# A two-layer decoder trunk: decay levels recorded four to a run, the second layer opened by the values of two groups, output pages split into other places and earlier

## The chip, the cores and the metric

The kernel runs on one core of one Trainium2 chip. The metric is the device time of one execution in microseconds (us). The engines are named as the profile names them: PE (TensorE, the matrix engine) with its weight loads PEld, DVE (VectorE), ACT (ScalarE), POOL (GpSimd), and SP (SyncE), whose queue issues every DMA of this kernel.

## The reference, cut to what matters

The input `x` has 1024 tokens of 1024 features. Layer A is gated linear attention with 4 heads (key width 128, value width 256), layer B is dilated sliding-window attention with 8 query heads in 3 groups over one shared set of keys and values. Each layer ends in an output projection, a residual and a layer norm.

```python
# layer A, per head, written chunk by chunk
b = cumsum(log_a)                                  # decay, log space, within a chunk
att[i, j] = sum_d q[i,d] * k[j,d] * exp(b[i,d] - b[j,d])      # j <= i
o = att @ v + (q * exp(b)) @ state
x1 = layer_norm(ALPHA * x + ((o / rms(o)) * g_norm * silu(g)) @ w_out)
# layer B
k, v = split(x1 @ w_kv)                            # 3 groups x 2 kv heads x 128
q, g = split(x1 @ w_in)
o_g = softmax over a band (windows 128, 512, 2048; dilations 1, 4, 16) per group
o = sum over groups of softmax(lse_g) * o_g
out = layer_norm(ALPHA * x1 + (o * silu(g)) @ w_out)
```

All of it is float32. The kernel gets float32 accuracy out of faster float32r matmuls by splitting each operand into a high and a low page (`split_hi` on ACT, `split_lo` on DVE or POOL) and issuing three matmuls, high by high, high by low and low by high.

## The kernel before, in words

Nothing is issued where it is written. Every call is recorded as an operation of a small scheduler, `Sched`, with a priority (its place in the text, moved by `S.later`), the engines that may run it (`S.vp` is DVE or POOL, `S.va` DVE or ACT) and an estimated cost. `Sched.order` then lets the operation that can start earliest go next, engine by engine, with buffers of a pool handed out in order. So an edit of the text changes the order on all engines, also far from the edit, and the order is fixed when the program is built. All instructions of the trace carry the helper's line, L452; tiles are told by their names.

Stages on PE, with the names of the tiles that it writes:

- Prologue, 1.25 to 29.9 us: values of head 0 and the gate's low rank (`pro`), while `x` arrives in tiles `xf` (tag `X`, 3 buffers) and is split to `xh`, `xl`.
- Layer A, to 337.8 us. Per head: projections of q, k and g (`acc`, 128x512), the gate (a matmul into `lv`, then `mn` on DVE and a scan into `b`), `levels`, `state_prep` (four-wide transposes of `ke` into `ms`), `chunks` (`po`, `ms`).
- Output projection of layer A with its layer norm, `out_ln(0, ...)`, first for tokens 0 to 511, then for 512 to 1023; it writes the pages `x1h`, `x1l` of layer B. The norm's two sums over features are pairs of matmuls with a page of ones, `ms<-sum,onesr`.
- Layer B, from 431.4 us: `layer_b` projects values and keys, then loops over 8 units (heads) with `scores`, `q_proj`, `g_proj`, `attend`, `close`.
- Output projection of layer B: tokens 0 to 511 by feature blocks (`out_ln(1, ...)`, banks `acc`, `lv`, `po` in turn), tokens 512 to 1023 by rows (`out_ln_rows`, weights `woh`, `wol`).

What the change touches:

- `levels(h)`, line 899. The attention matrix of a chunk is put together from eight small pieces: `k` against `q` for the diagonal, and for each L of 64, 32, ..., 1 a tile `X` that DVE, POOL and ACT fill (two subtractions, an exponential, two products), multiplied with itself. The products are float32 matmuls that use 32 columns of the array at a time (the trace writes them `128*32`, two records each). Two pieces at a time go into one bank, `lv` (2 buffers), as one group, so PE has four such groups per head, and DVE and ACT move each bank on to `Dg` and `AT`.
- `layer_b(xs)`, from line 1174. It starts with `proj_v0(range(4))`: values of group 0, four blocks of 128 tokens, each block a 256-wide `acc` accumulated over all eight pages of `x1`. `proj_v(0)` follows: values of groups 1 and 2 for tokens 0 to 511, four banks (`lv`, `lv`, `po`, `po`) at once, so that each page of `x1` is used by 12 matmuls of 512 columns before the next is needed.
- The end, lines 1553 to 1574. The gated output of each unit, `og`, is written to memory (`ogB`) for units 0 to 5, read back after the last `g_proj` through staging tiles `ogf` (tag `a`, 13 buffers, shared with the score tiles `P`) and split to `ogh`, `ogl` in pool `p1`, 16 pages that the `x1` pages leave. The weight pages `woh`, `wol` of the row part lie in pool `p0`.

Of the kernel before, what the change touches and what calls it, by code (L numbers as in the profile page):

```python
# [7 lines left out]
F32 = mybir.dt.float32  # L8
# [589 lines left out]
def trunk(tc, xT, wP, wA, wA12, wAv3, w2, wO, wK, wV0, wV12, wB, wOB, par_d,  # L598
# [13 lines left out]
    def split_hi(dst, src):  # L612
        S.scalar.activation(dst, src, AF.Copy)
# [4 lines left out]
    def page(pool, dt, name):  # L618
        return pool.tile([128, T], dt, name=name, tag="pg", bufs=16)

    def hs(half):
        return slice(half * 512, half * 512 + 512)
# [94 lines left out]
    def og_page(kt, pool):  # L717
        while kt >= len(ogs):
            n = len(ogs)
            a = page(pool, FR, f"ogh{n}")  # L720
            b = page(pool, FR, f"ogl{n}")
            ogs.append((a, b))
        return ogs[kt]

    def layer_a(t2, t1, after):
# [13 lines left out]
        S.vector.memset(smask.rearrange("p (n c) -> p n c", c=128)[:, :, 0:1], 0.0)  # L739

        def xtile(dt, name, shape=(128, T)):
            return t1.tile(list(shape), dt, name=name, tag="X", bufs=3)

        H = [dict() for _ in range(GH)]
        xs = []
# [137 lines left out]
        def gate(h):  # L883
            b = t1.tile([128, T], F32, name="b", tag="b", bufs=2)
            H[h]["b"] = b
            for half in range(2):
                r = hs(half)
                z = ps.tile([128, 512], F32, name="lv", bufs=2)
                S.tensor.matmul(z, w2t[:, h * 128:h * 128 + 128], aT[:, r], start=True, stop=True)
                sp = t1.tile([128, 512], F32, name="sp", bufs=2)  # L890
                S.scalar.activation(sp, z, AF.Abs, bias=b2c[:, h:h + 1])
                S.scalar.activation(sp, sp, AF.Exp, scale=-1.0)
                S.scalar.activation(sp, sp, AF.Ln, bias=onec)
                mn = t1.tile([128, 512], F32, name="mn", bufs=2)
                S.vector.tensor_scalar(mn, z, b2c[:, h:h + 1], 0.0, op0=OP.add, op1=OP.min)
                S.vp.tensor_sub(mn, mn, sp)
                S.vector.tensor_tensor_scan(b[:, r], smask, mn, 0.0, op0=OP.mult, op1=OP.add)

        def levels(h):
            q, k, b = H[h]["q"], H[h]["k"], H[h]["b"]  # L900
            AT, Dg = ATs[h % 2], Dgs[h % 2]
            pair = []

            for li in (NLEV - 1, *range(NLEV - 1)):
                if li < len(LEVELS):
                    L = LEVELS[li]
                    n = T // (2 * L)
                    X = xtile(F32, "X")
                    view = lambda t: t.rearrange("p (n s l) -> p n s l", s=2, l=L)
                    bv, Xv = view(b), view(X)  # L910
                    ref = bv[:, :, 0, L - 1:L].to_broadcast([128, n, L])
                    S.vector.tensor_sub(Xv[:, :, 1, :], bv[:, :, 1, :], ref)
                    S.vp.tensor_sub(Xv[:, :, 0, :], ref, bv[:, :, 0, :])
                    S.scalar.activation(X, X, AF.Exp, scale=1.0 / 16.0)
                    S.vector.tensor_mul(Xv[:, :, 1, :], Xv[:, :, 1, :], view(q)[:, :, 1, :])
                    S.vp.tensor_mul(Xv[:, :, 0, :], Xv[:, :, 0, :], view(k)[:, :, 0, :])
                    lt, rt = X, X
                else:
                    L = 0
                    lt, rt = k, q  # L920


                pair.append((li, L, lt, rt))
                if len(pair) < 2:
                    continue
                pb = ps.tile([128, 2, 256], F32, name="lv", bufs=2)
                with S.group():
                    for i, (_, L, lt, rt) in enumerate(pair):
                        for c in range(NCH):
                            o = c * 128  # L930
                            if L == 64:

                                for s in (0, 32):
                                    d = c % 2 * 64 + s
                                    S.tensor.matmul(pb[d:d + 32, i, c // 2 * 64:c // 2 * 64 + 64],
                                                     lt[:, o + s:o + s + 32], rt[:, o + 64:o + 128],
                                                     start=True, stop=True)
                                continue
                            for s in (0, 64) if L == 32 else range(0, 128, 32):
                                e = s + 32 if L == 32 else s  # L940
                                S.tensor.matmul(pb[s:s + 32, i, c * 32:c * 32 + 32], lt[:, o + s:o + s + 32],
                                                 rt[:, o + e:o + e + 32], start=True, stop=True)
                for i, (lj, L, _, _) in enumerate(pair):
                    if L == 64:
                        pl = pb[:, i].rearrange("p (c q) -> p c q", q=64)
                        AP = AT.rearrange("p (c two) i -> p two c i", two=2)
                        for x in range(2):
                            S.va.copy(AP[0:64, x, :, 64:128], pl[x * 64:x * 64 + 64])
                        continue
                    pl = pb[:, i].rearrange("p (c q) -> p c q", q=32)  # L950
                    if L == 32:
                        for s in (0, 64):
                            S.va.copy(AT[s:s + 32, :, s + 32:s + 64], pl[s:s + 32])
                    else:
                        S.vector.copy_predicated(
                            Dg, lmask[:, lj - 2:lj - 1, :].to_broadcast([128, NCH, 32]), pl)
                pair = []
            for s in range(0, 128, 32):
                S.va.copy(AT[s:s + 32, :, s:s + 32], Dg[s:s + 32])
# [91 lines left out]
    def small(name, tag, bufs, dt=F32, shape=(128, 512)):  # L1051
        return hp.tile(list(shape), dt, name=name, tag=tag, bufs=bufs)

    def load_og(src, kt, pool, stage, halves=(0, 1)):
        hi, lo = og_page(kt, pool)
        for half in halves:
            f = stage()
            S.sync.dma_start(f, src[:, hs(half)])
            split_hi(hi[:, hs(half)], f)
            split_lo(lo[:, hs(half)], f, hi[:, hs(half)])  # L1060
# [110 lines left out]
            return ap.rearrange("p (n a e) -> p n a e", n=4, a=8)  # L1171
        return ap.rearrange("p (i r) -> p i r", r=DIL[g])

    def layer_b(xs):
        bmask = hp.tile([128, 256], F32, name="bmask", bufs=1)
        S.sync.dma_start(bmask, bmask_d)
        rmask = hp.tile([128, 64], F32, name="rmask", bufs=1)
# [26 lines left out]
        def proj_v0(blocks):  # L1204
            for c in range(2):
                if V[c][0] is None:
                    V[c][0] = page(p0, F32, f"V{c}0")

            def evac(j, acc):
                S.scalar.activation(blk(V[0][0], j), acc[:, 0:128], AF.Copy)  # L1210
                S.vector.tensor_copy(blk(V[1][0], j), acc[:, 128:256])
            project_tok(wV0, xs, [(j, lambda x, j=j: blk(x, j)) for j in blocks], evac)
# [47 lines left out]
                S.sync.dma_start(x1t[i][:, et * 128:et * 128 + 128], blk(t, i))  # L1260


        proj_v0(range(4))
        proj_v(0)
        for g in range(3):
            for c in range(2):
                project(wK[2 * g + c], xs, lambda hf, acc, p=K[c][g]: rope(p, g, hf, acc))
# [40 lines left out]
        def g_proj(u):  # L1308
            sg = page(p0, F32, "sg")
            U[u]["sg"] = sg  # L1310

            def evac(half, acc):
                th = small("th", "t1", 2)
                S.scalar.activation(th, acc, AF.Tanh, scale=0.5)
                S.vector.scalar_tensor_tensor(sg[:, hs(half)], th, 1.0, acc, op0=OP.add, op1=OP.mult)
            project(wB[u, 3], xs, evac)
# [194 lines left out]
        for u in range(8):  # L1511
# [9 lines left out]
            if u == 3:  # L1521
                reload_kv()
        for u in (4, 5, 6, 7):
            g_proj(u)
            if u < 7:
                close(u)
# [22 lines left out]

    for half in range(2):  # L1550
        out_ln(0, hs(half), lambda et: load_w(wO[et]), lambda et: xT[et * 128:et * 128 + 128, :], emit_a)
    U = layer_b(x1s)

    ogs.clear()
    for kt in range(6):
        load_og(ogB[kt], kt, p1, lambda: small("ogf", "a", 13))
    for u in (6, 7):
        hi, lo = og_page(u, p1)
        for half in range(2):
            split_hi(hi[:, hs(half)], U[u]["og"][:, hs(half)])  # L1560
            split_lo(lo[:, hs(half)], U[u]["og"][:, hs(half)], hi[:, hs(half)])

# [4 lines left out]
    wo = []  # L1567
    for kt in range(NK):
        wf = wts.tile([128, 1024], F32, name="wf", bufs=2)
        hi, lo = page(p0, FR, "woh"), page(p0, FR, "wol")  # L1570
        with S.later(-EVAC):
            S.sync.dma_start(wf.rearrange("p (e c) -> p e c", e=NK), wOB[:, :, kt, :].rearrange("e p c -> p e c"))
            split_hi(hi, wf)
            split_lo(lo, wf, hi)
        wo.append((hi, lo))
# [96 lines left out]
```

## Time and profile before

| | us |
|---|---|
| median of 3 runs (1156.07 to 1156.78) | 1156.69 |
| the profiled execution's own time | 1157.39 |
| its span in the profile | 1155.6 |
| PE busy, share of the span | 1144.7, 99% |
| DVE busy | 808.5, 70% |
| ACT busy | 459.5, 40% |
| POOL busy | 199.6, 17% |
| first matmul of the program starts | 1.25 |
| last matmul of the program ends | 1148.0 |

The span is the stretch between the first and the last instruction of the profiled execution; 1.8 us lie around it. In a timeline row the first number is the start, the second the time from the start of its first to the end of its last instruction, both in us, and `x64` says that 64 records were merged. A matmul's own duration overlaps that of the next; what a matmul costs in a stream is the distance from its start to the next start. PE counts as busy while it is in such a stream, so a busy PE may still lose time: a distance longer than the usual one is how a wait or a change of work shows.

### The profile page before, as it was taken

How to read it: one execution, taken by the hardware profiler on the slowest of the kernel's cores; microseconds unless marked ns; L12 is line 12 of the kernel's file. 1: busy time of each engine (PE TensorE's matmuls, PEld its weight loads, DVE VectorE, ACT ScalarE, POOL GpSimd, SP SyncE). 2: the span in 40 equal slices, each digit the busy share in tenths (PEclk: the TensorE clock that was granted, in tenths of full speed). 3: DMA queues.
4: the chain of work that ended last, by engine and by line, in shares of the span. 5: the costliest groups of instructions: out<-in, count | busy, mean ns of one | idle time of the engine just before them, and what ended most of it. 6: DMA issues, size and time to landing. Idle time of an engine off the chain costs nothing.

```text
span 1155.6 us, 19794 instructions
## 1 busy us (share of the span) xinstructions
PE 1144.7 (99%) x7780; PEld 975.2 (84%) x7780; DVE 808.5 (70%) x1636; ACT 459.5 (40%) x965; POOL 199.6 (17%) x157
## 2 busy tenths in 40 slices
PE   9999999999999999999999999999999999999997
PEld 8888888889988888888888888888888888888876
DVE  6295952686966698765366868676778778768578
ACT  5354531545463335311214343434322433435242
POOL 1000000102111120221020314141222222204100
PEclk9999999999999999999999999999999999999999
DMA  8111122111144463643611211111151011124645
GB/s 266 59 39 37 67 81 86 43 57 46 66 170 135 141 199 134 200 135 111 210 37 38 56 38 56 38 40 53 38 165 39 20 39 37 39 75 146 199 129 183
DMA packets 93374, 108.40 MB, mean 94 GB/s; under 512 B 43648, under 2 KB 61952, under 8 KB 93280
## 3 DMA queue, kind: packets, MB, share of 16 engines
q1 hardware_dynamic: 93280, 107.13, 29.7%
q8 instruction: 61, 1.00, 0.4%
q14 instruction: 33, 0.27, 0.1%
HBM read 85.94 MB, written 21.17 MB: 93 GB/s over the span
## 4 chain that ended last, share of the span: by engine, by line
PE 93%; DVE 3%; DMA 2%; ACT 1%; issue 0%; SPq 0%; DVEq 0%
PE acc L452 63%; PE po L452 9%; PE lv L452 8%; PE vac L452 8%; PE ms L452 4%; PE pro L452 2%; DMA wf<-in_wOB 2%; DVE rt L452 1%; DVE wl L452 1%; DMA xf<-in_xT 1%; DVE wol L452 0%; DVE x1l L452 0%; ACT woh L452 0%; ACT wh L452 0%; SPq L452 0%
## 5 line engine op out<-in xcount | busy, mean ns | idle before, releaser
L452 PE MATMUL acc<-x1h,wh 128*128 128x512 f32 x608 | 252.1, 415 | 0.0
L452 PE MATMUL acc<-x1h,wl 128*128 128x512 f32 x608 | 237.6, 391 | 0.0
L452 PE MATMUL acc<-x1l,wh 128*128 128x512 f32 x608 | 237.0, 390 | 0.0
L452 ACT ACTIVATE wh<-wf 128x1024 fp32r<-128x1024 f32 (+2 forms) x104 | 108.2, 1041 | 260.9 <-PE acc L452 158.8
L452 POOL TENSOR_TENSOR wl<-wf,wh 128x1024 fp32r<-128x1024 f32 x43 | 102.9, 2394 | 564.3 <-ACT wh L452 366.9
L452 PEld LDWEIGHTS acc<-x1h,wl 128*128 128x128 f32 x608 | 114.1, 188 | 24.8
L452 PEld LDWEIGHTS acc<-x1l,wh 128*128 128x128 f32 x608 | 114.5, 188 | 21.3
L452 PEld LDWEIGHTS acc<-x1h,wh 128*128 128x128 f32 x608 | 114.4, 188 | 21.0
L452 ACT ACTIVATE P<-P,sts 128x128 f32<-128x128 f32 (+2 forms) x192 | 81.5, 425 | 121.8 <-DVE sts L452 121.4
L452 DVE TENSOR_TENSOR wl<-wf,wh 128x1024 fp32r<-128x1024 f32 (+2 forms) x62 | 76.9, 1240 | 57.7 <-ACT wh L452 45.6
L452 PE MATMUL acc<-xh,wh 128*128 128x512 f32 x256 | 101.9, 398 | 0.0
L452 PE MATMUL acc<-xh,wl 128*128 128x512 f32 x256 | 99.8, 390 | 0.0
L452 PE MATMUL acc<-xl,wh 128*128 128x512 f32 x256 | 99.7, 389 | 0.0
L452 DVE TENSOR_TENSOR t<-acc,cosT 128x512 f32<-128x512 f32 x60 | 41.3, 689 | 65.1 <-PE acc L452 65.0
L452 DVE TENSOR_TENSOR t<-acc,sinT 64x512 f32<-64x512 f32 x120 | 82.6, 688 | 1.6
L452 PE MATMUL lv<-K,Q 128*64 128x64 f32 (+2 forms) x512 | 69.4, 286 | 0.0
L452 DVE CUSTOM_DVE_ANT_0 P<-lv,bmask 128x256 f32<-128x256 f32 (+1 forms) x128 | 46.4, 379 | 29.3 <-PE lv L452 28.5
L452 DVE TENSOR_TENSOR Q<-t,t 128x512 f32<-128x512 f32 x44 | 61.7, 1402 | 1.3
L452 PEld LDWEIGHTS lv<-K,Q 128*128 128x128 f32 (+1 forms) x512 | 53.2, 163 | 10.0 <-issue 1.1
L452 PE MATMUL acc<-ogh,wh 128*128 128x512 f32 x152 | 60.2, 396 | 0.0
L452 PE MATMUL acc<-ogl,wh 128*128 128x512 f32 x152 | 59.2, 389 | 0.0
L452 PE MATMUL acc<-ogh,wl 128*128 128x512 f32 x152 | 59.2, 389 | 0.0
(251 smaller groups left out, 2227.8 us busy)
## 6 DMA issues: line engine op xcount, KB each, us to landing
wf<-in_wB SPq DMA_DIRECT2D x32, 512.0 KB
wf<-in_wA SPq DMA_DIRECT2D x24, 512.0 KB
wf<-in_wO SPq DMA_DIRECT2D x16, 512.0 KB
wf<-in_wOB SPq DMA_DIRECT2D x16, 512.0 KB
wf<-in_wV SPq DMA_DIRECT2D x12, 512.0 KB
res<-in_xT SPq DMA_DIRECT2D x16, 256.0 KB
x1d<-rt SPq DMA_DIRECT2D x16, 256.0 KB
out<-rt SPq DMA_DIRECT2D x16, 256.0 KB
```

What stands on the lines that cost most here:

```text
L452: getattr(handle[o.eng], meth)(*[conv(a) for a in args], **{k: conv(v) for k, v in kw.items()})
```

## The change

Three places, and what the scheduler makes of them everywhere else.

1. `levels`: four pieces are gathered before a group is recorded, so the group holds four pieces, in two banks `lv`. For that a fourth buffer of the tag `X` is made, in the room of the tile `mn`, whose steps now work in `b` itself.
2. `layer_b`: `proj_v(0)` is recorded ahead of `proj_v0(range(4))`.
3. The end: a function `early`, called ahead of the last `g_proj`, reads and splits `ogB` of units 0 to 3, half page by half page, into pages of pool `p0` (places that Q and K have left). Units 4 to 7 follow after layer B into `p1`. The first four pairs of weight pages `woh`, `wol` go to `p1` instead of `p0`.

The work on PE is the same, matmul for matmul.

```diff
-            return t1.tile(list(shape), dt, name=name, tag="X", bufs=3)
+            return t1.tile(list(shape), dt, name=name, tag="X", bufs=4)
...
-                mn = t1.tile([128, 512], F32, name="mn", bufs=2)
-                S.vector.tensor_scalar(mn, z, b2c[:, h:h + 1], 0.0, op0=OP.add, op1=OP.min)
-                S.vp.tensor_sub(mn, mn, sp)
-                S.vector.tensor_tensor_scan(b[:, r], smask, mn, 0.0, op0=OP.mult, op1=OP.add)
+
+                S.vector.tensor_scalar(b[:, r], z, b2c[:, h:h + 1], 0.0, op0=OP.add, op1=OP.min)
+                S.vp.tensor_sub(b[:, r], b[:, r], sp)
+                S.vector.tensor_tensor_scan(b[:, r], smask, b[:, r], 0.0, op0=OP.mult, op1=OP.add)
...
-                if len(pair) < 2:
+                if len(pair) < 4:
                     continue
-                pb = ps.tile([128, 2, 256], F32, name="lv", bufs=2)
+                pbs = [ps.tile([128, 2, 256], F32, name="lv", bufs=2) for _ in range(2)]
                 with S.group():
-                    for i, (_, L, lt, rt) in enumerate(pair):
+                    for j, (_, L, lt, rt) in enumerate(pair):
+                        pb, i = pbs[j // 2], j % 2
...
-    def layer_b(xs):
+    def layer_b(xs, early):
...
+        proj_v(0)
         proj_v0(range(4))
-        proj_v(0)
...
         for u in (4, 5, 6, 7):
+            if u == 7:
+                early()
             g_proj(u)
...
-    U = layer_b(x1s)
-
-    ogs.clear()
-    for kt in range(6):
-        load_og(ogB[kt], kt, p1, lambda: small("ogf", "a", 13))
-    for u in (6, 7):
-        hi, lo = og_page(u, p1)
+
+    def early():
+        ogs.clear()
         for half in range(2):
+            for kt in range(4):
+                with S.later(-EVAC):
+                    load_og(ogB[kt], kt, p0, lambda: small("ogf", "a", 13), (half,))
+
+    U = layer_b(x1s, early)
+    for half in range(2):
+        for kt in range(4, 6):
+            load_og(ogB[kt], kt, p1, lambda: small("ogf", "a", 13), (half,))
+        for u in (6, 7):
+            hi, lo = og_page(u, p1)
             split_hi(hi[:, hs(half)], U[u]["og"][:, hs(half)])
...
-        hi, lo = page(p0, FR, "woh"), page(p0, FR, "wol")
+        q = p1 if kt < 4 else p0
+        hi, lo = page(q, FR, "woh"), page(q, FR, "wol")
```

What the scheduler makes of the first part on PE, in head 0 of layer A, before the change (`lv` rows are the small pieces, `ms<-ident,ke` the transposes of `state_prep`; the `acc` rows between are left out):

```order
L452 MATMUL lv<-q,k 32x32 x32
L452 MATMUL lv<-X 32x64 x16
...
L452 MATMUL lv<-X 32x32 x48
...
L452 MATMUL lv<-X 32x32 x64
...
L452 MATMUL lv<-X 32x32 x64
L452 MATMUL ms<-ident,ke 128x128 x8
```

And with it, the same place:

```order
L452 MATMUL lv<-q,k 32x32 x32
L452 MATMUL lv<-X 32x64 x16
L452 MATMUL lv<-X 32x32 x48
...
L452 MATMUL lv<-X 32x32 x128
...
L452 MATMUL ms<-ident,ke 128x128 x8
```

Four stretches of small pieces have become two in this head, and the transposes, which stood right behind the last stretch, now stand alone with `acc` matmuls on both sides. Heads 1, 2 and 3 have the same rows.

The second place is DVE at the end of layer A's layer norm for tokens 512 to 1023, from the last two additions of its running sum `lnA`. Before:

```order
L452 TENSOR_TENSOR lnA<-lnA,rt 128x512 x2
L452 COPY V_4478<-acc 128x128
L452 TENSOR_TENSOR sum<-lnA,sum 128x512
L452 COPY V_4478<-acc 128x128
L452 TENSOR_TENSOR rt<-rt,mean 128x512 x2
```

With the change:

```order
L452 TENSOR_TENSOR lnA<-lnA,rt 128x512 x2
L452 TENSOR_TENSOR sum<-lnA,sum 128x512
L452 TENSOR_TENSOR wl<-wf,wh 128x1024
L452 TENSOR_TENSOR rt<-rt,mean 128x512 x4
L452 TENSOR_TENSOR sq_4487<-sq_4487,sq_4493 128x512
```

More than 50 rows ahead of these are the same in both programs. On PE the first `ms<-sum,onesr` pair stood behind 60 matmuls of 256 columns (`acc`) and now stands behind 33 of 512 columns (`vac`); the second stood behind another 36 of 256 and 57 of 512 columns and now stands behind another 63 of 512.

The third place is SP's queue near the end, around the last unit's weights `cw`, which `attend(7)` needs. Before:

```order
L452 DMA cwd_9732<-ew 8x8x8 x4
L452 DMA wf<-in_wOB 128x1024
L452 DMA cw<-cwd_9732 128x8x1
L452 DMA cw<-cwd_9732 128x2x4
L452 DMA ogf<-ogB_6951 128x512 x2
```

With the change:

```order
L452 DMA ogf<-ogB_7485 128x512
L452 DMA ogf<-ogB_8053 128x512
L452 DMA cwd_9739<-ew 8x8x8 x4
L452 DMA wf<-in_wOB 128x1024
L452 DMA ogf<-ogB_6401 128x512
L452 DMA cw<-cwd_9739 128x8x1
L452 DMA ogf<-ogB_6943 128x512
L452 DMA cw<-cwd_9739 128x2x4
```

Two half-page loads more stand ahead of the writes of `cwd`, and two more ahead of the last read of `cw`.

More of the change, by code (lines that the diff above doesn't have):

```diff
@@ L942, in levels @@
                                                  rt[:, o + e:o + e + 32], start=True, stop=True)
-                for i, (lj, L, _, _) in enumerate(pair):
+                for j, (lj, L, _, _) in enumerate(pair):
+                    pb, i = pbs[j // 2], j % 2
                     if L == 64:
```

## The prediction

> **What bounds the kernel now.** I read the page first, then the chain of work that ended last, then who waited on PE, then PE's timeline where starts lie further apart than usual.
>
> ```profile
> PE 1144.7 (99%) x7780; PEld 975.2 (84%) x7780; DVE 808.5 (70%) x1636; ACT 459.5 (40%) x965; POOL 199.6 (17%) x157
> ...
> PE 93%; DVE 3%; DMA 2%; ACT 1%; issue 0%; SPq 0%; DVEq 0%
> ```
>
> PE is busy in 1144.7 of 1155.6 us and makes up 93% of the chain, so the end moves by what PE's stream gains or loses, and by nothing else unless another engine gets so late that PE runs dry. The waits that the profile sees on PE:
>
> ```profile
> PE pro L452 <- DVE Dg L452: 1.2, 1, 1.2
> PE acc L452 <- DVE x1l L452: 0.6, 1, 0.6
> PE acc L452 <- DVE wol L452: 0.6, 1, 0.6
> PE pro L452 <- ACT xh L452: 0.4, 2, 0.2
> PE acc L452 <- DVE rt L452: 0.2, 1, 0.2
> ```
>
> The 1.6 us of the prologue (`pro`) the change leaves in place, and beside them there are 1.4 us. What else PE loses lies in distances between starts. In a plain stream of 512-column matmuls the distance is 21.76 / 96 = 0.227 us, from this row of the chain:
>
> ```profile
> 186.91 21.76 PE acc L452 x96
> ```
>
> The work on PE is the same with the change, so three places decide: the stretches of small pieces in layer A, the start of layer B, and the end.
>
> **Part 1, joined stretches.** PE's timeline in head 0 around stretches of small pieces (three places), and around full-array transposes and products near the end (two places):
>
> ```profile
> 69.56 0.76 PE L452 MATMUL lv<-q,k 128*32 128x32 f32 x64
> 70.17 0.65 PE L452 MATMUL lv<-X 128*32 128x64 f32 x32
> ...
> 82.31 0.39 PE L452 MATMUL acc<-xh,wl 128*128 128x512 f32 x1
> 82.62 1.37 PE L452 MATMUL lv<-X 128*32 128x32 f32 x128
> 83.92 0.50 PE L452 MATMUL acc<-xh,wh 128*128 128x512 f32 x1
> 84.25 0.39 PE L452 MATMUL acc<-xl,wh 128*128 128x512 f32 x1
> ...
> 89.27 0.39 PE L452 MATMUL acc<-xh,wl 128*128 128x512 f32 x1
> 89.58 1.37 PE L452 MATMUL lv<-X 128*32 128x32 f32 x128
> 90.88 1.09 PE L452 MATMUL ms<-ident,ke 128*128 128x128 f32 x8
> 91.73 0.47 PE L452 MATMUL acc<-xh,wh 128*128 128x512 f32 x1
> 92.04 0.39 PE L452 MATMUL acc<-xl,wh 128*128 128x512 f32 x1
> ...
> 1047.41 0.39 PE L452 MATMUL acc<-x1h,wl 128*128 128x512 f32 x1
> 1047.64 1.03 PE L452 MATMUL ms<-ident,P 128*128 128x128 f32 x8
> 1048.43 0.48 PE L452 MATMUL acc<-ogh,wh 128*128 128x512 f32 x1
> 1048.74 0.39 PE L452 MATMUL acc<-ogl,wh 128*128 128x512 f32 x1
> ...
> 1055.05 0.61 PE L452 MATMUL po<-PT,V 128*128 128x128 f32 x4
> 1055.41 0.47 PE L452 MATMUL lv<-ogh,wh 128*128 128x512 f32 x1
> ```
>
> Inside a stretch 64 pieces take 70.17 - 69.56 = 0.61 us, 9.5 ns each, with the step from one piece's level to the next in it. A stretch of 128 between two `acc` streams takes 84.25 - 82.31 = 1.94 us, from the last matmul before it to the second one after it. Two of these distances are ordinary (0.45), the pieces are 128 x 9.5 = 1.22, and 0.27 are left: the price of having a stretch at all. For full-array work, eight records before an `acc` take 1048.43 - 1047.64 = 0.79 and four take 1055.41 - 1055.05 = 0.36, so 0.43 / 4 = 0.108 each; the whole place at 1047.41 is 1.33 - 0.45 - 0.86 = 0.02. Full-array float32 work may be set among the fast matmuls at no price, and what costs is the 32-column form. The stretch with transposes behind it costs 2.77 - 0.45 - 1.22 - 0.86 = 0.24.
>
> Per head there are now three stretches at 0.27 and one at 0.24, 1.05 us. With the change there are two at 0.27, and the transposes alone at 0.02, 0.56 us. Four heads: 4 x 0.49 = 2.0 us less. Bounds: 8 x 0.08 - 4 x 0.05 = 0.4 if only the way in is saved (82.62 - 82.31 less 0.227 is 0.08; the transposes on their own cost 0.05 more than behind pieces), and 8 x 0.27 = 2.2 at the other end. I take 2.0, since its rows are this very work.
>
> The joined run has to wait for four pieces instead of two. Today the second stretch of head 0 starts close behind its last input:
>
> ```profile
> 73.37 0.69 DVE L452 TENSOR_TENSOR X<-X,k 128x512 f32<-128x512 f32 x1
> ...
> 74.38 1.27 PE L452 MATMUL lv<-X 128*32 128x32 f32 x96
> ```
>
> The input ends at 74.06, 0.32 us before the start. The joined run stands behind 72 `acc` matmuls where the first stretch stood behind 54: 69.56 + 18 x 0.227 = 73.6. DVE has no bank to empty before it any more, but fills two halves of the next piece (about 0.6 each) earlier, so the input ends near 73.7. I cost that at nothing; where it fails is a rival. Emptying two banks instead of one before the next run is hidden: that run is 51 matmuls away, 11.6 us. The scan in `b`, the fourth `X` and the DMA order in the prologue move nothing on PE: its first matmuls that wait for `x` come ahead of the place where the order changes.
>
> **Part 2, the start of layer B.** PE's rows there, the sums on DVE among them:
>
> ```profile
> 431.38 0.28 PE L452 MATMUL acc<-wh,x1h 128*128 128x256 f32 x1
> ...
> 433.42 0.28 PE L452 MATMUL acc<-wh,x1l 128*128 128x256 f32 x1
> 433.81 0.38 PE L452 MATMUL acc<-wh,x1h 128*128 128x256 f32 x1
> 434.03 0.28 PE L452 MATMUL acc<-wl,x1h 128*128 128x256 f32 x1
> 434.93 0.39 PE L452 MATMUL acc<-wh,x1l 128*128 128x256 f32 x1 [0.62 <-DVE x1l L452]
> 435.52 0.39 PE L452 MATMUL acc<-wh,x1h 128*128 128x256 f32 x1 [0.21 <-DVE rt L452]
> 435.75 0.28 PE L452 MATMUL acc<-wl,x1h 128*128 128x256 f32 x1
> ```
>
> ```profile
> 439.23 0.69 DVE L452 TENSOR_TENSOR sum<-lnA,sum 128x512 fp32r<-128x512 f32 x1 [0.50 <-ACT sum L452]
> ...
> 456.71 0.69 DVE L452 TENSOR_TENSOR sum<-sq,sum 128x512 fp32r<-128x512 f32 x1 [0.70 <-ACT sum L452]
> ```
>
> A block of `proj_v0` eats a page of `x1` in three matmuls, 0.36 us, faster than DVE makes one. From 433.42 to 435.75 five distances take 2.33 us where five of 0.12 would do: 1.73 us lost. `proj_v(0)` eats a page in 12 x 0.227 = 2.7 us, so this loss goes. What is late next is the norm's first sum: PE comes to it after 33 matmuls, 431.38 + 7.49 = 438.87, while DVE's low half, whose queue ahead is the same, ends at 439.92. The pair can end near 440.2 instead of 439.3, and the first matmul after a wait costs another 0.1 (435.75 - 435.52 against 0.12): 1.0 us lost. The second sum comes 63 matmuls (14.3 us) later, near 454.6. DVE now needs 456.71 + 0.69 - 439.92 = 17.5 us from the first sum to the end of the second; with the change it has no copies of `V` between (about 0.4 less), one weight split moves into its wait for the mean and another falls behind (about 2.5 less, by 1.23 each), and one addition comes from POOL (0.6 more): about 15.2, so 455.1, and some of the 0.7 and 0.8 that it idles for ACT goes too. I count 0.1 lost there. Net 1.73 - 1.1 = 0.6 less; bounds 1.7 less (neither sum late) and 0.6 more (DVE as slow as today, 1.3 at the second sum).
>
> **Part 3, the end.** Splitting pages of units 0 to 3 early gives PE finished work among the steps of `attend(7)`. What it loses there now is small:
>
> ```profile
> 1052.71 1.80 PE L452 MATMUL po<-PT,V 128*128 128x128 f32 x12
> 1054.27 0.48 PE L452 MATMUL acc<-ogh,wh 128*128 128x512 f32 x1
> ...
> 1111.26 0.39 PE L452 MATMUL acc<-woh,ogh 128*128 128x512 f32 x1
> 1112.22 0.50 PE L452 MATMUL acc<-wol,ogh 128*128 128x512 f32 x1 [0.57 <-DVE wol L452]
> ```
>
> Twelve records at 0.108 less the short last one (0.07) are 1.23 us, and the distance is 1.56: 0.33 lost. I take 0.3 less. The loss at 1111.26 (0.96 - 0.227 = 0.73) waits for a weight page whose load is paced by transfers and by PE's own progress, and PE's order from there on is unchanged; I leave it. SP issues four half-page loads earlier, two of them ahead of the last read of `cw`; near nothing while PE has other work, and bounds of 1 less and 1 more.
>
> **The sum.** 2.0 + 0.6 + 0.3 = 2.9 us less: 1157.39 - 2.9 = 1154.5 for an execution like the profiled one, which lies 0.7 above the median, and 1156.69 - 2.9 = 1153.8 against the median. About 0.2%, 2.3 us, is what a measurement of this kernel can tell from no change; the line is 1154.4.
>
> **Rivals.**
>
> *Neither sum is late*: 1.1 us more goes, 1152.7. For it: the sums are pushed on PE only by the order. Against it: DVE has no idle time ahead of the first. 0.11.
>
> *The joined runs wait for their inputs.* The slack at 74.38 was 0.32 us, and a run of four pieces has the latest of four. 0.25 us at each of eight runs takes back 2.0: 1155.8. For it: that slack; against: the scheduler sets other `acc` matmuls ahead. 0.17. [...]
>
> *Only the way in is saved*, because the rest of the 0.27 belongs to pieces and goes with them: 0.4 + 0.6 + 0.3, 1155.4. For it: within the stretch the distance can't be seen piece by piece. 0.10. [...]
>
> *Slower: `attend(7)` comes late.* SP stands on a half-page load that waits for a staging tile, the reads of `cw` stand behind it, and DVE has splits ahead of the scaling of `P`. PE's other work there is 18 groups of three (12.2 us). It decides from the point where the last page of unit 7 is later than that work lasts; 5 us past it cost 5 us: 1156.7 - 2.6 + 5 = 1159.1. Against it: the splits of unit 7's second half no longer stand ahead of the first. 0.06.
>
> **How the numbers follow.** My forecast has 0.56, with 1153.1 to 1154.5 of its own, nine in ten of it under the line. Faster: 0.5 + 0.11 = 0.61. Slower by over 0.2%: 0.06. No change that can be told: 0.33. The range runs from 1152.2, both sums in time and the end better by another half, to 1156.0, with the waiting inputs in it.
>
> **What would show it.** Right: eight stretches of small pieces, each as long as its pieces and 0.27; no distance over 0.2 us in the first 33 matmuls of layer B, then about 1 us at the first `ms<-sum`; 0.7 still lost at a `wol`. Wrong: distances of 0.3 and more ahead of `lv` runs; stretches of 192 and 256 pieces longer than 9.5 ns a piece; idle PE between the last `g_proj` and the first product with unit 7's page.

## The result, and the profile after

| | before | after |
|---|---|---|
| median, us (4 runs each) | 1156.59 (1156.07 to 1156.78) | 1167.65 (1166.55 to 1169.70) |
| profiled execution, us | 1157.39 | 1167.26 |
| its span, us | 1155.6 | 1165.4 |

The changed kernel is slower: ratio 1.0097, 95% interval 1.0082 to 1.0112, 11.1 us. The forecast was 1153.8 in a range of 1152.2 to 1156.0. (Of all executions of all kernels below, one of the twelve of e5 is far off, 5167.56 us; it counts as slow and its ratio leaves it out.) From the page of the changed kernel, the busy time, the DMA queue that brings instructions, and the shares of the chain:

```profile
PE 1144.6 (98%) x7780; PEld 977.2 (84%) x7780; DVE 816.3 (70%) x1637; ACT 458.1 (39%) x967; POOL 195.1 (17%) x154
...
q8 instruction: 61, 1.00, 0.3%
...
PE 93%; DVE 3%; issue 1%; ACT 1%; DMA 0%; SPq 0%; DVEq 0%
```

PE is busy as long as before (1144.7) in a span that is 9.8 us longer, so PE stands idle for 9.8 more. The page shows it only as 1% of "issue", time in which an engine waits for nothing that the profile shows. Where it lies, by the first matmuls of each stage in the two traces:

| stage, up to | before, us | after, us | the stage's change |
|---|---|---|---|
| layer A and its output projection, to the first matmul with `x1` | 431.38 | 444.07 | +12.69 |
| start of layer B, to the first `lv<-K,Q` | 607.81 | 619.76 | -0.74 |
| units, to the last `lv<-K,Q` | 1023.59 | 1035.52 | -0.02 |
| end, to the end of the span | 1155.62 | 1165.41 | -2.14 |

So the start of layer B and the end became shorter, by 0.74 where 0.6 was forecast and by 2.14 where 0.3 was, and layer A became longer. (How much of the 2.14 is the change's own is asked under part 3 below.) What PE waited for in the changed kernel (us in all, times, longest):

```profile
PE lv L452 <- issue: 9.6, 5, 2.5
PE ms L452 <- DVE S L452: 1.7, 1, 1.7
PE pro L452 <- DVE Dg L452: 1.2, 1, 1.2
PE lv L452 <- DVE S L452: 0.5, 1, 0.5
PE ms L452 <- DVE sum L452: 0.2, 1, 0.2
PE ms L452 <- ACT sum L452: 0.2, 1, 0.2
```

The first row is new and the largest. PE's timeline at its five places, all inside joined runs of small pieces (heads 0, 1, 2, and both runs of head 3):

```profile
87.60 2.23 PE L452 MATMUL lv<-X 128*32 128x32 f32 x219
92.29 0.76 PE L452 MATMUL lv<-X 128*32 128x32 f32 x37 [2.46 <-issue]
...
153.11 2.67 PE L452 MATMUL lv<-X 128*32 128x32 f32 x253
157.38 0.25 PE L452 MATMUL lv<-X 128*32 128x32 f32 x3 [1.60 <-issue]
...
259.47 2.28 PE L452 MATMUL lv<-X 128*32 128x32 f32 x222
264.08 0.47 PE L452 MATMUL lv<-X 128*32 128x32 f32 x34 [2.33 <-issue]
...
307.30 1.59 PE L452 MATMUL lv<-X 128*32 128x64 f32 x116
310.40 0.28 PE L452 MATMUL lv<-X 128*32 128x32 f32 x10 [1.50 <-issue]
...
324.31 1.74 PE L452 MATMUL lv<-X 128*32 128x32 f32 x171
327.71 0.95 PE L452 MATMUL lv<-X 128*32 128x32 f32 x85 [1.67 <-issue]
```

After 219 of 256 pieces PE stops for 2.46 us, in the middle of one group whose inputs have long been there: no engine and no transfer of data is named. From start to start the five distances are 2.65, 1.80, 2.53, 1.70 and 1.86 us, 10.5 in all. The three other joined runs (the first ones of heads 0, 1 and 2, 192 records each) have no stop.

What goes on around the first of them is seen in the transfers of the whole core from 89 to 94 us (the first row is the window in 40 slices of 0.125 us):

```profile
DMA  0000000040000000000000000000000000600000
...
q8 instruction: 2, 0.03, 2.8%
```

Nothing moves on the core but two packets of the instruction queue, the first at 90.0 us, just after PE stopped. PE goes on 2.3 us after that packet starts, and so it is at the other four stops: packets start at 155.1, 261.7, 308.0 and 325.5, and PE goes on 2.2 to 2.4 us later. The page has 61 such packets and 7780 + 7780 matmuls and weight loads, 15560 / 61 = 255 instructions to a packet if all are PE's; e9 and e13 below, with 1024 records of each kind more, have 69, one more for each 256 instructions (nine move in each one's dense stretch of 1152 records). A piece, counted as in the timeline rows, is one record of each kind. So by estimate a packet holds 128 pieces, which at 9.5 ns each last 1.22 us, and a packet of plain 512-column matmuls lasts 128 x 0.227 = 29 us.

### The profile page after: what moved, and what is told of

Its sections match the earlier page's. It is cut to its first block, busy times and chain, and to the rows that moved or that the text cites. A ratio compares the mean times of both kernels' runs of the same rounds, so it can differ in the third digit from the quotient of the medians.

```text
span 1165.4 us, 19779 instructions
## 1 busy us (share of the span) xinstructions
PE 1144.6 (98%) x7780; PEld 977.2 (84%) x7780; DVE 816.3 (70%) x1637; ACT 458.1 (39%) x967; POOL 195.1 (17%) x154
## 4 chain that ended last, share of the span: by engine, by line
PE 93%; DVE 3%; issue 1%; ACT 1%; DMA 0%; SPq 0%; DVEq 0%
PE acc L452 62%; PE lv L452 9%; PE po L452 9%; PE vac L452 7%; PE ms L452 3%; PE pro L452 2%; DVE rt L452 1%; DVE wl L452 1%; DVE ogl L452 0%; DVE x1l L452 0%; DMA ogf<-ogA 0%; ACT wh L452 0%; DVE lnA L452 0%; SPq L452 0%; ACT ogh L452 0%
## 5 line engine op out<-in xcount | busy, mean ns | idle before, releaser
L452 POOL TENSOR_TENSOR wl<-wf,wh 128x1024 fp32r<-128x1024 f32 x41 | 98.2, 2396 | 555.0 <-ACT wh L452 363.8
L452 DVE TENSOR_TENSOR wl<-wf,wh 128x1024 fp32r<-128x1024 f32 (+2 forms) x64 | 81.2, 1271 | 61.6 <-ACT wh L452 51.7
```

The costliest lines, as they stand in the source:

```text
L452: getattr(handle[o.eng], meth)(*[conv(a) for a in args], **{k: conv(v) for k, v in kw.items()})
```

## The experiments

**Theory F**, drawn from these packets: PE's instructions come in blocks of 256, and a block of nothing but small pieces is used up faster than the next can be brought, so PE stops at the end of a block. **Rivals**: the run itself stops PE, by its change of bank half way, a late input or the array's narrow form (B); the loss is an effect of the other parts, or of the fourth `X` and the scan in `b`, on the order of DVE's work (A; in the later expectations G is the fourth `X` with the scan, H the other parts).

Each kernel's median beside that of the kernel before on the same chip:

| kernel | what it is | us | before, us | ratio, 95% interval |
|---|---|---|---|---|
| e1 | change with pairs again | 1158.06 | 1156.82 | 1.0008 (0.9999 to 1.0017) |
| e2 | joined runs alone | 1170.75 | 1156.82 | 1.0119 (1.0102 to 1.0137) |
| e3 | change, 40 records more ahead | 1173.26 | 1156.82 | 1.0142 (1.0128 to 1.0156) |
| e4 | change, filled runs | 1167.24 | 1156.82 | 1.0090 (1.0074 to 1.0105) |
| e5 | start of layer B and end | 1155.48 | 1156.69 | 0.9991 (0.9982 to 1.0000) |
| e6 | start of layer B alone | 1156.48 | 1156.69 | 0.9997 (0.9988 to 1.0005) |
| e7 | end alone | 1156.35 | 1156.69 | 0.9995 (0.9986 to 1.0004) |
| e8 | fourth `X`, scan in `b` | 1159.45 | 1156.69 | 1.0021 (1.0013 to 1.0030) |
| e9 | dense stretch, one quarter | 1191.43 | 1157.23 | one execution |
| e10 | e5, four first runs joined | 1158.00 | 1157.23 | 1.0006 (0.9997 to 1.0015) |
| e11 | e5, three first runs joined | 1154.48 | 1157.23 | 0.9979 (0.9970 to 0.9988) |
| e12 | scan in `b` alone | 1157.19 | 1157.23 | 1.0002 (0.9993 to 1.0011) |
| e13 | dense stretch, four quarters | 1188.27 | 1157.20 | one execution |

### The stops: e2, e3, e4, e9, e13

**e2**, the joined runs without the rest of the change (`if len(pair) < 4` with its two banks, the fourth `X`, the scan in `b`, on the kernel before).

> The kernel before with four levels to a run (with the fourth X and the scan in b that this needs) and nothing else of the change. Theory F: the instruction stream of layer A is the changed kernel's, so the same five stops stand at the same pieces (218, 252 and 222 of 256, 182 of 192, 171 of 256), 10.5 us of them; layer A and its out-projection cost 12.7 more, and the 1.7 at the start of layer B and the 0.7 at a wol stay: 1169.3 (1168 to 1170.5). Rival (the stops come from the earlier loads or another order of the later parts): under 1165.

It took 1170.75, 0.25 above the upper end. Its four executions lie in two pairs, 1168.42 and 1168.90 with a mean granted clock of 0.997, 1172.60 and 1172.94 with 0.993 and 0.995. The five stops stand after the same pieces, with other lengths (2.29, 1.80, 2.05, 1.87, 2.40 us). The later parts have no share in them.

**e3**, the blocks' ends moved.

```diff
             for _ in range(WARM):
                 S.tensor.matmul(accs[7][:, 0:256], ...)
...
+            for _ in range(20):
+                S.tensor.matmul(accs[7][0:32, 0:32], Dgs[0][:, 0, :], Dgs[0][:, 1, :], start=True, stop=True)
```

> The changed kernel with 20 more matmuls of 32 x 32 (40 records, 80 instructions, about 0.4 us) among the warming ones ahead of everything; their result is written over. Every other instruction keeps its order. Theory F: the ends of the blocks lie 40 records earlier in every run, so each stop moves with them: in the second runs to about pieces 178, 212, 181 and 130 of 256, in the first runs to about 165 (head 0), 172 (head 2) and 141 (head 3) of 192, with head 1's at the very end or gone; 7 stops instead of 5, 4 us more: 1172 (1170 to 1174). Rival B (the run itself stops PE: the change of bank in the middle, a late input, a wait of the array): the same five stops at the same pieces, 1168.0 (1167 to 1169).

1173.26, in F's range and far from B's. That the time itself fits is in part luck: of the 6.3 us between the profiled executions of e3 and of the changed kernel only 3.2 lie between the first `acc` and the first matmul with `x1`; 1.7 lie ahead of the first `acc` and 1.4 at the end. The places are the test. PE's timeline in e3, the two runs of head 0, the second run of head 2, and the place behind head 3's second run:

```profile
75.89 1.50 PE L452 MATMUL lv<-X 128*32 128x64 f32 x104
79.19 0.40 PE L452 MATMUL lv<-X 128*32 128x32 f32 x24 [1.80 <-issue]
...
91.29 1.88 PE L452 MATMUL lv<-X 128*32 128x32 f32 x179
95.41 1.06 PE L452 MATMUL lv<-X 128*32 128x32 f32 x77 [2.23 <-issue]
...
264.95 1.88 PE L452 MATMUL lv<-X 128*32 128x32 f32 x183
269.33 0.86 PE L452 MATMUL lv<-X 128*32 128x32 f32 x69 [2.49 <-issue]
...
333.05 0.40 PE L452 MATMUL acc<-xl,wh 128*128 128x512 f32 x1
334.90 0.40 PE L452 MATMUL acc<-xh,wl 128*128 128x512 f32 x1 [1.45 <-issue]
```

The stops after 219 and 222 pieces are now after 179 and 183: 40 earlier (39 in head 2), as many records as were put ahead. Head 0's first run, which had none, stops at 168 (64 + 104). Counted from the start of the program, stops stand after matmul records 858, 1623, 2512, 3023 and 3279 in the changed kernel, which lie 765, 889, 511 and 256 apart, all within 7 of a multiple of 128. In e3 three of them stand after records 858, 1623 and 2513, though other pieces are there. The place belongs to the instruction stream, not to the pieces.

Two of the places forecast were missed, both in head 3: there the ends of blocks lay about 15 and 3 pieces into a run, and the blocks that began there made no full stop (0.4 us in the first run, none in the second; the next end came just behind the run and stopped `acc` matmuls, the last row above). The trace shows that these two came sooner: the instruction packets start at 313.6 and 326.7, ahead of the runs, which begin at 313.95 and 330.25, while at every full stop the packet starts inside the run. Why they came sooner was not tested by itself.

**e4**, the second runs stretched with other work.

```diff
+                        if j == 2 and L < 16:
...
+                            for _ in range(12):
+                                S.tensor.matmul(pb[:, 0, 0:128], ident, ident, start=True, stop=True)
```

> The changed kernel with 12 more float32 matmuls of 128 x 128 (24 records, 2.6 us) in the middle of each second run, written over by the pieces behind them: 10.4 us more work for PE in all. Theory F: a block with these records in it takes 104 x 0.0095 + 2.6 = 3.6 us, about what the next one needs, so the four stops in the second runs shrink to under 0.5 and the added work costs next to nothing there; each run's blocks also move by 24 records a head, so that in the first runs head 3's stop goes and head 2 gets one near piece 164. Time 1169.3 (1168 to 1171). Rival B: the stops stay and the work adds up: 1178 (1176.5 to 1179).

1167.24, below F's range (from 1168): 10.4 us more work for PE, and the time is that of the changed kernel. Head 0's second run and the only stop that was left, in head 2's first run:

```profile
87.17 1.36 PE L452 MATMUL lv<-X 128*32 128x32 f32 x128
88.46 2.94 PE L452 MATMUL lv<-ident 128*128 128x128 f32 x24
91.33 1.36 PE L452 MATMUL lv<-X 128*32 128x32 f32 x128
...
245.67 1.40 PE L452 MATMUL lv<-X 128*32 128x64 f32 x97
248.63 0.45 PE L452 MATMUL lv<-X 128*32 128x32 f32 x29 [1.55 <-issue]
```

From 87.17 to the `acc` behind the run are 5.5 us here and were 5.4 in the changed kernel (87.60 to 92.97), with 2.6 us of work in the place of the stop. As forecast, head 3's first run lost its stop and head 2's got one. Two differences from the changed kernel go with its coming out below the forecast: in the profiled executions the wait of `ms` for `S` is 0.5 instead of 1.7, and the mean granted clock is 0.999 instead of 0.996 (0.998 to 0.999 in all four of e4, 0.995 to 0.997 there). What each is worth was not measured.

**e9** and **e13**, one stretch of 1152 records in head 0 of the kernel before. Their added line (e13; in e9 all 512 went to `pb[0:32, 0, 0:32]`):

```diff
+                        for n in range(512):
+                            s, o = n % 4 * 32, n // 4 % 8 * 128
+                            S.tensor.matmul(pb[s:s + 32, ...], lt[:, o + s:o + s + 32], rt[:, o + s:o + s + 32], ...)
```

> The kernel before with 512 more small matmuls (1024 records) ahead of the 128 records of head 0's last run, into the same place, written over by the pieces behind them: one stretch of 1152 records, 9 blocks of 256 instructions. Theory F: PE goes through a block in 1.2 us and then stands until the next is there; from the stops so far (1.7 to 2.65 us after 1.22 us of work) 2.9 to 3.9 us for each block, so 8 stops 128 records apart and 25 to 33 us for the stretch. Rival B: 1152 records of 9.5 ns and no stop that comes back every 128, 11 to 13 us.

> As e9_dense, but the 512 added matmuls go through the four quarters in turn, as the real pieces do (in e9_dense all stood in one quarter and took 31.7 ns a record, so a block lasted 4.05 us and no stop came back). Now a record takes 9.5 ns and a block of 128 records 1.22 us. Theory F: PE stops every 128 records, 8 or 9 times in the 1152; with 2.9 to 3.9 us from block to block the stretch takes 24 to 33 us, and the blocks arrive that far apart. Rival C (a stop belongs to the join of two banks or comes once in a run, whatever its length): 11 to 14 us with one stop or none.

e9 missed both: 34.8 us, and one stop near the end. PE's timeline in e9:

```profile
89.34 33.41 PE L452 MATMUL lv<-X 128*32 128x32 f32 x1115
123.64 0.53 PE L452 MATMUL lv<-X 128*32 128x32 f32 x37 [0.89 <-issue]
```

The added pieces stood in one quarter of the array and took 31.7 ns a record, so a block lasted 4.05 us, and PE did not stop until record 1115, among the kernel's own pieces. So 1115 records of the narrow form in a row brought no stop by themselves. In e13, with the same pieces spread over the four quarters:

```profile
88.94 2.05 PE L452 MATMUL lv<-X 128*32 128x32 f32 x219
93.28 1.63 PE L452 MATMUL lv<-X 128*32 128x32 f32 x128 [2.29 <-issue]
97.00 1.94 PE L452 MATMUL lv<-X 128*32 128x32 f32 x128 [2.10 <-issue]
100.46 1.93 PE L452 MATMUL lv<-X 128*32 128x32 f32 x128 [1.52 <-issue]
...
119.65 0.75 PE L452 MATMUL lv<-X 128*32 128x32 f32 x37 [1.80 <-issue]
```

Eight stops, exactly 128 records apart, and 31.4 us for the stretch: both as F has them, and the rival of e13 (one stop or none) fell. From 93.28 to 119.65 seven blocks take 26.4 us, 3.8 each (3.5 to 4.0). The granted clock there is 0.50 from 93.9 on (0.53 over 93 to 110, 0.50 over 110 to 124), and a block's own work takes up to 1.7 us instead of 1.22. In the changed kernel, where it was 1.00 on the way into each stop, PE goes on 3.0 to 3.9 us after it began the block before (128 records back). So in these two kernels PE got its next block 3.0 to 4.0 us after the one before, and in e9, where a block had 4.05 us of work, no stop stands among the added pieces.

### The rest of layer A: e1, e8, e12

**e1**, the changed kernel with pairs.

```diff
-                if len(pair) < 4:
+                if len(pair) < 2:
...
-                pbs = [ps.tile([128, 2, 256], F32, name="lv", bufs=2) for _ in range(2)]
+                pbs = [ps.tile([128, 2, 256], F32, name="lv", bufs=2) for _ in range(1)]
```

> The changed kernel with two levels to a run of small pieces again; the start of layer B and the end stay as changed. Theory F (instruction fetch): PE stops inside a joined run because its instructions, two for each record, arrive in blocks of 256, and a block of nothing but small pieces (128 records, 1.22 us) is used up faster than the next one can be brought. Runs of 96 and 128 records don't hold a whole block beside the work around them, so no stop is left: no wait of PE for 'issue' over 0.3 us, the wait of 1.7 us for S in the last head goes too, and with the 0.7 that the start of layer B and the 1.7 that the end gained the time is 1154.2 (1153.4 to 1155.2). Rival A (the loss in layer A comes from the fourth X, the scan in b or another order on DVE): the stops are gone or not, but layer A still ends 2 to 10 us late, 1156.5 or more.

No stop is left, but the time is 1158.06, not 1154.2: layer A still ends late, the first matmul with `x1` at 434.85 against 431.38. Rival A is right about this part. **e8** puts only the fourth `X` and the scan in `b` on the kernel before, **e12** only the scan.

> The kernel before with only the fourth X and the scan in b, two levels to a run as before. Theory G: DVE's order in layer A moves and PE waits for X or S in the last head, 3.4 us: 1160 (1158.5 to 1161). Theory H, or no effect: 1156.7.

> The kernel before with only the scan in b (mn gone, three X as before). Theory G splits here: if the fourth X alone moved DVE's order, 1156.7 (1156.0 to 1157.3); if the scan in b does it, 1159.5.

e8 took 1159.45 and e12 1157.19, so it is the fourth buffer that costs about 2.5 us (ratio 1.0021); in e8's trace the first matmul with `x1` stands at 434.44, 3.06 later than before. DVE's timeline in e8 in the last head, and PE's at the same place:

```profile
333.51 1.33 DVE L452 TENSOR_TENSOR ogl<-ogf,ogh 128x512 fp32r<-128x512 f32 x2 [2.42 <-ACT ogh L452]
334.76 0.69 DVE L452 COPY sg<-acc 128x512 f32<-128x512 f32 x1
335.36 0.42 DVE L452 COPY S<-ms 128x256 f32<-128x256 f32 x1
```

```profile
335.83 0.38 PE L452 MATMUL po<-qe,S 128*128 128x128 f32 x1 [0.53 <-DVE S L452]
```

With a fourth `X` the scheduler sets the page splits `ogl` elsewhere in DVE's queue: one that waits 2.42 us for ACT stands ahead of the copy of `S`, and PE waits for that. This place loses 0.7 us from start to start, and is not alone: between 316 and 357 us further distances on PE are longer than usual by 0.6 (for an `X`), 0.3 (for `S` again), 0.4 (for an `ogl`) and 0.6 (at the norm's first sums), 2.6 in all of the 3.06. In the changed kernel two distances that end with `S` are longer by 1.9 and 0.7 (`PE ms <- DVE S` and `PE lv <- DVE S` in the waits above).

### The start of layer B, the end, and a faster version: e5, e6, e7, e10, e11

> The kernel before with only the new start of layer B and the new end; layer A as before (two levels to a run, three X, the piece mn). Theory G: what the run with pairs lost (3.5 us between the last run and layer B) belongs to the fourth X and the scan in b, which put DVE's work in another order; without them layer A takes as long as before, and the 0.7 at the start of layer B and the 1.5 to 1.7 at the end are left: 1154.4 (1153.6 to 1155.2). Rival H (the loss comes from the later parts, through their loads or their pages): layer B again begins 3 us late, 1157.5.

> The kernel before with only the two calls at the start of layer B exchanged. From the changed kernel's trace: 0.7 less at the start of layer B, with the first sum still 0.9 late, and nothing else: 1156.0 (1155.3 to 1156.8). Theory H: 3 more.

> The kernel before with only the pages of units 0 to 3 split early. From the changed kernel's trace: 0.5 less around the last attention unit and 1.1 less at the wol, whose wait goes: 1155.1 (1154.3 to 1156.0). As the prediction had it (0.3 less, the wait for wol stays): 1156.4. Theory H: 3 more.

Together the two parts make 1155.48, 1.2 us less, with an interval that ends at 1.0000; each alone gave 0.2 and 0.3 less, which a measurement of this kernel can't tell from nothing. e6 lies in its range; e5 and e7 came out 0.3 and 0.35 above the upper ends of theirs, so the end is worth less than its 2.14 in one pair of traces made me expect. Layer B begins at 431.05 in e5, as before, so H falls.

**e10** and **e11** are e5 with four levels joined where a run has 192 records only (`size = 4 if h in (0, 1, 2, 3) else 2`, in e11 `(0, 1, 2)`, and `size = 2` after the first group of a head).

> The kernel before with the new start of layer B and the new end, and with four levels joined only in the first run of each head (192 records); the rest in pairs, three X, mn as before. Counting records, the ends of blocks fall at about 77, 111, 84 and 55 (and 183) of 192 in heads 0 to 3. Theory F: only head 3's run has a whole block of pieces inside it and stops, 1.7 us, near piece 182; each join saves 0.4: 1155.5 - 1.6 + 1.7 = 1155.6 (1154.8 to 1156.6). Theory G adds, if DVE's order moves in the last head: up to 3 more.

> As e10_first4, but head 3 in pairs throughout. Theory F: no stop at all, three joins save 0.4 each: 1155.5 - 1.2 = 1154.3 (1153.5 to 1155.2), the fastest of all these kernels. Rival (joining saves nothing once the stops are gone): 1155.5. If the joined runs wait for their inputs with three X: 1156 or more and a wait of PE's lv for X.

e11 is the fastest kernel here, 1154.48, in its range and 2.7 us less than the kernel before, with only those joins in it that bring no stop; its waits on PE:

```profile
PE pro L452 <- DVE Dg L452: 1.2, 1, 1.2
PE ms L452 <- ACT sum L452: 0.2, 1, 0.2
PE ms L452 <- DVE sum L452: 0.2, 1, 0.2
```

Up to the first matmul with `x1`, from the first `acc`, e11 takes 1.27 us less than e5 (400.28 against 401.55), 0.42 for each join; in the five kernels that have layer A in pairs and three `X` this stretch takes 401.47 to 401.67. e10 differs by one join, that of head 3, whose run holds a whole block:

```profile
299.78 1.22 PE L452 MATMUL lv<-X 128*32 128x64 f32 x91
302.98 0.32 PE L452 MATMUL lv<-X 128*32 128x32 f32 x11 [1.98 <-issue]
```

The stop is where it was forecast (near 182; 181 here), but it costs more than the 1.7 that I took: 2.2 from start to start, and behind it the granted clock is 0.53 for 3.6 us in the profiled execution. That one is the slowest of e10's ten (1160.87, mean clock 0.997). The seven with a mean clock of 0.998 or 0.999 take 1156.83 to 1158.23, and the median, 1158.00, lies above the range, which ended at 1156.6; the clock is part of that, and the rest was not found.

## Why the prediction was wrong, point by point

**Part 1, the step that failed.** The prediction took 9.5 ns for a piece from a stretch of 64 records and carried it to runs of 192 and 256: "Four heads: 4 x 0.49 = 2.0 us less". In head 0's run of 256 it held as far as piece 219, where PE stopped (2.23 us); from the start of that run to the `acc` behind it are 5.37 us, 21 ns a piece. Its own sign of error came true ("stretches of 192 and 256 pieces longer than 9.5 ns a piece"). The kernel before has no such stop (the waits on PE name no "issue"): its longest run has 128 records, and a block has slow matmuls in it unless it begins exactly with the run.

The saving itself is there, and somewhat larger than forecast. The 12.7 us of layer A are 10.5 of stops, 3.1 of the fourth `X` (e8's stage), by estimate 1.5 of slow clock after the first stop (3.0 us at 0.50, below; 512-column matmuls stand 0.43 us apart there), and so about -2.4 for the joins, where 2.0 was forecast and 2.2 was the bound. Counted at the runs themselves, as the prediction counts a stretch's price, it is about 2.5: a stretch of 96 costs 0.49 or more in heads 0 to 2 and not the 0.27 of a stretch of 128, a joined run of 192 costs 0.55 to 0.61, and a joined run of 256 without its stop about 0.25. e11's 0.42 for a join agrees with the first two.

**"The scan in `b`, the fourth `X` and the DMA order in the prologue move nothing on PE"** failed for the fourth `X`: about 2.5 us in e8, nothing in e12, which has the scan alone. It rested on PE's first matmuls and left out DVE's order in the last head.

**Inputs and banks.** The forecast that joined runs don't wait for their inputs, and that two banks are emptied in time, held: the waits name no `X` and no bank in the changed kernel. The rival that they wait fell.

**Part 2** was right in its mechanism, and nearly in its size. No distance is long in the first 33 matmuls of layer B, and the first sum is late as forecast, while the second, where 0.1 was counted, is not. PE's rows in the changed kernel:

```profile
451.32 0.39 PE L452 MATMUL vac<-wh,x1l 128*128 128x512 f32 x1
451.94 0.49 PE L452 MATMUL ms<-sum,onesr 128*128 128x512 f32 x1 [0.23 <-ACT sum L452]
452.67 0.50 PE L452 MATMUL ms<-sum,onesr 128*128 128x512 f32 x1 [0.23 <-DVE sum L452]
...
467.30 0.63 PE L452 MATMUL ms<-sum,onesr 128*128 128x512 f32 x2
```

The two distances of the first sum are 0.9 us longer than ordinary ones (1.0 forecast), and the stage gained 0.74 (0.6 forecast; 0.42 in e5 and e6, with layer A as before).

**Part 3** looks larger than the 0.3 in this pair of traces: from the last `lv<-K,Q` to the end 2.1 us went, 0.55 of it up to the row part, 0.5 behind the last matmul, and 1.1 in the row part, most of it at a `wol`, whose wait the prediction left in place:

```profile
1122.62 0.39 PE L452 MATMUL acc<-woh,ogh 128*128 128x512 f32 x1
1122.85 0.39 PE L452 MATMUL acc<-wol,ogh 128*128 128x512 f32 x1
```

These are the two matmuls that stood 0.96 apart, now 0.23. But e7, which has this part alone, is only 0.3 faster by the medians, and the wait comes and goes from trace to trace: it is missing in e8, whose end is as before, and 0.8 us in e10, which has the new end. From the last `lv<-K,Q` to the end the seven traces with the old end take 130.9 to 132.8 us, the eight with the new one 129.9 to 132.8, 0.8 less on average. So the 2.1 is in part chance, and that this part gained more than the 0.3 is not shown. The rival in which `attend(7)` comes late fell; it was the only slower one, and the cause that came was not among the rivals.

## What to carry to other kernels

Here a rate measured over a short stretch of tiny instructions (9.5 ns over 64 records) did not carry to a long one (21 ns over 256): count the instructions of a run. Where 256 of PE's (128 matmuls with their loads) made up about 1.2 us of work, PE stopped (two blocks of e3 aside); where they lasted 4.05 us (e9), or slower work stood among them, as between the pairs and in e4's second runs, it did not. Stops marked "issue", each with an instruction packet that starts 2.2 to 2.9 us before PE goes on (2.2 to 2.4 in the changed kernel, 2.4 to 2.9 in e13), were the sign; that they kept their count from the start of the program when work was put ahead (e3) was the test. And one more buffer was a change of DVE's order that cost about 2.5 us (e8): look at what it puts ahead of what, at the place where the next engine waits.

## What the runs showed of the hardware that was not expected

In the changed kernel 61 instruction packets stand beside 15560 matmuls and weight loads, 255 to a packet. A dense block of 128 pieces is about 1.22 us of work (an estimate from 9.5 ns a piece), and PE went on with the next one only 3.0 to 3.9 us after it began the one before in the changed kernel, 3.5 to 4.0 in e13.

Pieces that go through the four quarters in turn took 8.5 ns a record in e13 ahead of its first stop (219 in 2.05 us, less 0.2 for the last record's own length; 9.5 in the prediction's row), in one quarter 31.7 (e9).

Behind some stops the granted clock fell. The changed kernel ahead of and behind its first stop, and behind its third, and then e13 among its stops (busy time with counts, then the granted clock, which is the third number from the end):

```profile
90.00:92.20 2.20, 0.00 (x0) 0.00 (x0) 0.00 (x0) 0.00 (x0) 0.00 (x0) 0.93 0.03 7
92.20:95.20 3.00, 2.91 (x42) 2.45 (x43) 0.54 (x1) 0.97 (x2) 0.00 (x0) 0.50 0.03 5
...
264.00:267.00 3.00, 2.92 (x45) 2.45 (x45) 2.00 (x3) 1.38 (x4) 0.00 (x0) 1.00 0.15 56
...
110.00:120.00 10.00, 4.61 (x314) 4.22 (x306) 0.00 (x0) 0.00 (x0) 0.00 (x0) 0.50 0.02 3
```

After 2.46 us of idle time the clock was 0.50 for 3 us, after 2.33 us elsewhere it stayed at 1.00; in e13, where 1.5 to 2.3 us of idle time came in every block, it was 0.50 to the end of the stretch. Why it fell behind one stop and not behind another was not shown.

Open is also why an instruction packet starts sooner at one place and later at another (stops of 1.5 to 2.5 us at like places), and what in the fourth `X` decides the scheduler's order; no run was made for either.
